# Sums of down weights moved ahead of the attention, roots and broadcasts moved forward by the scheduler, and another order in the last quarter

## The chip, the core and the metric

The kernel runs as one program on one core of a Trainium2 chip. The core has a matrix engine (TensorE, in the profile PE, with its weight loads as PEld), three engines for element-wise work (VectorE = DVE, ScalarE = ACT, GpSimd = POOL) and SyncE (SP), which here issues nearly all transfers between the chip's large memory and the core's own memory (SBUF). Matmuls write into banks of a small accumulator memory (PSUM). The metric is the device time of one execution in microseconds (us), as the median of several runs.

## What is computed

One layer of a decoder trunk on 1024 tokens of width 1024, all in fp32. Cut to what matters here:

```python
def reference(x, mem, ...):
    h = rmsnorm(x, g_mix_pre)
    y_ssm, y_gmlp = s5_group(h @ w_in...), gmlp_group(h @ w_in...)
    x = x + rmsnorm(concat(y_ssm, y_gmlp) @ w_out, g_mix_post)
    h = rmsnorm(x, g_x_pre); mem_n = rmsnorm(mem, g_mem)
    # 4 heads of 256, 256 memory tokens
    x = x + rmsnorm(softmax(q k^T / 16) v @ w_o, g_x_post)
    h = rmsnorm(x, g_ffn_pre)
    val, gate = split(causal_conv3(h @ w_up))            # 2 x 2816 columns
    x = x + rmsnorm((val * gelu(gate)) @ w_down, g_ffn_post)
    return x

def rmsnorm(x, g):
    return x * rsqrt(mean(x * x, axis=-1) + 1e-6) * g
```

## The kernel before

**Layout.** All activations lie transposed: 128 features on the partitions, tokens along the free axis. The 1024 tokens are two halves of 512 (h = 0 and 1); a tile is 128x512 fp32, 256 KB. Every fp32 product is made of three matmuls: each operand is split into a rounded high part (a cast on ACT, L131 for weights, L252 for activations) and the rest (a subtraction on DVE, L134 and L253; L253 is on POOL for some), and `mm3` (L233) multiplies high by high, high by low and low by high. So each weight tile that SP loads (L85, `raw`) needs an ACT row and a DVE row before PE can use it.

**Stages.** In order of time: the two mixers (to about 330 us of the span), the out-projection `o1` of half 0 and of half 1 (to about 428), attention of half 0 and its projection `o2`, attention of half 1 and its `o2` (to about 660), up-projection with convolution (to about 1125), down-projection by a scheme of seven products in place of eight, which needs sums of weight blocks (to about 1310), and the tail, in which the last of these products is finished in two column quarters of 256 tokens.

**Norms.** `rms` sums squares over the features by eight or four narrow matmuls against a column of ones (L278, each 128x1), DVE turns the sum into a mean (L281), and `rsqrt` makes the inverse root by an integer guess and three Newton steps (DVE L261, L263, L269, L270: ten rows in all). `bcast` spreads the root over the partitions by matmuls against the identity (L305) into the PSUM bank `st`, and ACT copies it to SBUF (L308). `post` is the step behind a projection: times gain and broadcast (DVE L723), plus the residual (POOL L724), squares (ACT L709) and their sum (POOL or DVE L710).

**Sums of weights.** `s_sums` loads four tiles of w_down for each k of 0..10 into the pool `m` (L1350), makes four sums from them on POOL (L1354) and stores these to `sd` (L1355). It is a generator. The attention takes 14 of its steps in half 0 and the last 8 in half 1, so 28 and 16 of the 44 sums.

**Attention.** For a head: `q_block` (projection by w_q), `scores` (DVE takes the maximum, L1123, scales it by the root, L1124; ACT takes the exponential, L1128; DVE divides, L1132), `turn` (PE transposes the probabilities, L1142) and `weigh` (times v). The root for half 1 is scaled at L739.

**Tail.** `one` is one product of a quarter. While the first quarter of columns (11 k x 4 b) runs, the generator `job` squares the results of half 0 and calls `finish`: norm, broadcast, eight multiplications (DVE L766), eight residual adds (POOL L767) and the stores to the output (L769). In the second quarter (4 b x 11 k) `rms` of the first quarter's columns is called at TAIL_R and its broadcast at TAIL_B; `finish_pair` (L774, L776) multiplies and adds two row blocks at a time; L1515, L1516 are the quarter's squares and their sum.

**What sets the order.** The program is written in one order, and a scheduler then sorts each engine's instructions by an estimate of when they can run, weighing in a priority, which follows the place in the program. `tc.high_priority(n)` gives what is written under it the priority of n places earlier. `self.pin(...)` keeps rows in the order of the program while `self.pinned` is set. Tiles come from pools with a fixed number of slots (here `m` 16, `t` 11, `b` 32), and an instruction that writes a slot waits until its last reader is done.

Of the kernel before, what the change touches and what calls it, by code (L numbers as in the profile page):

```python
# [19 lines left out]
ALU = mybir.AluOpType  # L20
AX = mybir.AxisListType

P = 128
D = 1024
KT = 8
HALF = 512
NG = 32
EPS = 1e-6
# [9 lines left out]
POST_A = 0.8  # L38
POST_2B = 1
S5_RATE = 1.5  # L40
WARM = 10
EARLY = 1
MIX_AT = 2
Q_STATS = 3
TAIL_R = (1, 1)
TAIL_B = (1, 9)
T_FROM = 11
T_RATE = 1
FETCH = 2
# [102 lines left out]
class Builder:  # L152
# [102 lines left out]

    def rsqrt(self, x, shape, e=None):

        v = e or self.nc.vector
        y = self.tiny(shape, f"rs_y{shape[1]}", 1 if shape[1] == 64 else 4)
        t = self.tiny(shape, f"rs_t{shape[1]}", 1)  # L260
        self.pin(v.tensor_scalar(y.bitcast(I32), x.bitcast(I32), -0.5, 1597463007.0, ALU.mult, ALU.add))  # L261
        for _ in range(3):
            self.pin(v.tensor_tensor(t, y, y, ALU.mult))  # L263
            if e:
                e.tensor_tensor(t, t, x, ALU.mult)
                e.tensor_scalar(t, t, -0.5, 1.5, ALU.mult, ALU.add)
                e.tensor_tensor(y, y, t, ALU.mult)
                continue
            self.pin(v.scalar_tensor_tensor(t, t, -0.5, x, ALU.mult, ALU.mult))  # L269
            self.pin(v.scalar_tensor_tensor(y, t, 1.5, y, ALU.add, ALU.mult))  # L270
        return y

    def rms(self, acc, nt):

        nc = self.nc
        ps = self.bank("st")
        for i in range(nt):
            self.pin(nc.tensor.matmul(ps[:, i:i + 1], lhsT=acc[:, i * P:(i + 1) * P], rhs=self.ones[:, 0:1],  # L278
                                      start=True, stop=True))
        x = self.tiny([P, nt], "st_x", 2)  # L280
        self.pin(nc.vector.tensor_scalar(x, ps[:, :nt], 1.0 / D, EPS, ALU.mult, ALU.add))  # L281
        return self.rsqrt(x, [P, nt])

    def token_rms(self, name, nt, tag):

        nc = self.nc
        ss = self.tiny([P, 2, nt], f"ss_{name}", 1)
        for i in range(nt):
            for j in range(2):
                t = self.slot(tag)  # L290
                nc.sync.dma_start(t, self.a[name][i][:, j])
                nc.scalar.activation(t, t, AF.Square, accum_out=ss[:, j, i:i + 1])
            yield
        x = self.tiny([P, nt], f"sx_{name}", 1)
        g = nc.gpsimd
        g.tensor_tensor(x, ss[:, 0], ss[:, 1], ALU.add)
        g.tensor_scalar(x, x, 1.0 / D, EPS, ALU.mult, ALU.add)
        return self.rsqrt(x, [P, nt], g)

    def bcast(self, r, nt, tag="st"):  # L300

        nc = self.nc
        ps = self.bank("st")
        for i in range(nt):
            self.pin(nc.tensor.matmul(ps[:, i * P:(i + 1) * P], lhsT=r[:, i:i + 1].to_broadcast([P, P]),  # L305
                                      rhs=self.ident, start=True, stop=True))
        bc = self.slot(tag)
        nc.scalar.copy(bc[:, :nt * P], ps[:, :nt * P])  # L308
        return ps, bc

    def stats(self, acc, nt):
# [443 lines left out]
    def finish(self, m, acc, h, x2d):  # L755

        nc, v, g = self.nc, self.nc.vector, self.nc.gpsimd
        res = []
        for i in range(KT):
            t = self.slot("rs")  # L760
            nc.sync.dma_start(t, x2d[i][h])
            res.append(t)
        r, bc = yield from self.stats(acc, 4)
        for i in range(KT):
            x = m[i]
            v.scalar_tensor_tensor(x, x, self.gain["g_ffn_post"][:, i:i + 1], bc, ALU.mult, ALU.mult)  # L766
            g.tensor_tensor(x, x, res[i], ALU.add)  # L767
            yield
            nc.sync.dma_start(self.out[P * i:P * i + P, HALF * h:HALF * h + HALF], x)  # L769

    def finish_pair(self, x, res, bc, i, h, c0, e):

# [275 lines left out]
    def attention(self):  # L1048
        nc, a, w, ids = self.nc, self.a, self.w, self.ids
        v, g = nc.vector, nc.gpsimd  # L1050
# [37 lines left out]
        sq1 = [None, None]  # L1088
        xres = lambda i, hh: a["xT"][P * i:P * i + P, HALF * hh:HALF * hh + HALF]
        post = [None, None]  # L1090
        kv = self.side(kv_parts(), 1)
        for h in range(2):
            for b in range(8):
                proj(lambda k, hh: self.mix[k, hh], "o1", m1, sq1, b, h, (4, 5, 6, 7, 0, 1, 2, 3))
            for k in range(8):
                del self.mix[k, h]
            post[h] = self.post(m1[h], sq1[h], "g_mix_post", xres, h, "q", lambda i, hh: self.x1d[i][hh])
            if h == 0:
                self.drain(kv)
                self.side(post[0])  # L1100
# [56 lines left out]
        m2 = self.m2 = [[None] * 8, [None] * 8]  # L1157
        sq2 = [None, None]
        self.post2 = [None, None]
        s_job = self.s_sums()  # L1160
        for h in range(2):
            heads = lambda k, hh: oT[hh][k]
            for i in range(6):
                if i > 1:
                    next(s_job, None)
                if i == 5:
                    for b in range(EARLY):
                        begin(heads, "o2", b, h, range(6))
                if i == 1:
                    self.drain(post[h])  # L1170
                if 1 <= i <= 4:
                    scores(h, i - 1)
                for j in range(2):
                    if i:
                        next(s_job, None)
                    if i < 4:
                        q_block(h, i, j)
                    if i >= 2:
                        turn(i - 2) if j == 0 else weigh(h, i - 2)
            self.xg[h] = []  # L1180
            if h == 0:
                self.side(post[1])
            for b in range(8):
                proj(heads, "o2", m2, sq2, b, h)
            oT[h] = None
            self.post2[h] = self.post(m2[h], sq2[h], "g_x_post", lambda i, hh: self.x1d[i][hh], h, "f",
                                      lambda i, hh: self.x2d[i][hh])
            if h == 0:
                while not self.ready[1]:
                    next(post[1])  # L1190
                self.side(self.post2[0], POST_A)
            else:
                self.drain(self.post2[0])
# [148 lines left out]
    def s_sums(self):  # L1342

        nc, g = self.nc, self.nc.gpsimd
        for k in range(11):
            t = {}
            for o in range(2):
                for j in range(2):
                    t[o, j] = self.slot("m")
                    nc.sync.dma_start(t[o, j], self.a["w_dk"][k + 11 * j][:, HALF * o:HALF * o + HALF])  # L1350
            yield

            def put(n, to, x, y, op=ALU.subtract):
                g.tensor_tensor(t[to], t[x], t[y], op)  # L1354
                nc.sync.dma_start(self.sd[n][k], t[to])  # L1355

            put(1, (1, 1), (1, 0), (1, 1), ALU.add)
            put(3, (1, 0), (0, 0), (1, 0))
            put(2, (0, 0), (1, 1), (0, 0))
            put(4, (0, 1), (0, 1), (0, 0))  # L1360
            yield
# [80 lines left out]
    def down(self):  # L1442
# [69 lines left out]
        def squares(b, q):  # L1512
# [2 lines left out]
            self.pin(nc.scalar.activation(s, A[b][:, c], AF.Square))  # L1515
            self.pin(v.tensor_tensor(sq[1][:, c], sq[1][:, c], s, ALU.add))  # L1516

        for k in range(11):
            self.d_prep(44 if k > 5 else 39 + k)
            parts.append((self.dp.pop((33 + k, 0)), self.dp.pop((33 + k, 1))))  # L1520
            for b in range(4):
                one(k, b, quarters[0])
                if k == 10:
                    squares(b, 0)
                    out_part(4 + b, 0, A[b][:, quarters[0]])
            next(job, None)
        self.drain(job)
        st = {}
        for b in range(4):
            self.pinned = b > 0  # L1530
            for k in range(11):
                one(k, b, quarters[1])
                if (b, k) == TAIL_R:
                    st["r"] = self.rms(sq[1][:, quarters[0]], 2)
                if (b, k) == TAIL_B:
                    bc = self.bcast(st["r"], 2)[1]
                    for i in (3, 2):
                        self.drain(self.finish_pair(mg[0][i], res[0][i], wide(bc), i, 1, 0, g))
                    st["out"] = self.chain(*(self.finish_pair(mg[0][i], res[0][i], wide(bc), i, 1, 0, v)
                                             for i in (0, 1)))  # L1540
                if (b, k) > TAIL_B and k % 3 == 0:
                    next(st["out"], None)
            if b == 3:
                self.drain(st["out"])
            squares(b, 1)
            out_part(4 + b, 1, A[b][:, quarters[1]])
# [77 lines left out]
```

## Time and profile before

| | us |
|---|---|
| three runs | 1373.46, 1376.73, 1373.87 |
| median | 1373.87 |
| the profiled execution | 1375.64 |
| its span | 1373.8 |
| mean granted clock of PE in it | 0.967 of full |
| PE / DVE / POOL / ACT busy | 1275.9 / 1066.1 / 694.6 / 628.0 |

The span runs from the first to the last instruction of the profiled execution; the execution's own time is 1.8 us longer. All rows of a timeline are in us from the span's start: start, duration of the group, engine, line of the kernel, operation, tile written <- tiles read, shape, and in brackets the idle time of the engine ahead of the group with the instruction that ended it. A row of the waits is: waiting engine, tile and line, the releaser, then the total, the count, and the longest. A row of the windows is: the stretch and its length, busy time of PE, PEld, DVE, ACT and POOL (with counts), the granted clock of PE, the share in which the DMA engines were busy, and GB/s.

### The profile page before, as it was taken

To read this page: it belongs to the slowest core of one execution; us is meant where nothing else is said; L and a number is where in the kernel's file an instruction comes from. 1 tells how busy PE (TensorE), PEld (TensorE's weight loads), DVE (VectorE), ACT (ScalarE), POOL (GpSimd) and SP (SyncE) were. 2 spreads that over 40 slices of the span, in tenths; PEclk is the share of its full clock that TensorE was granted. 3 is DMA by queue.
4 is the path that set the end of the run, shared out by engine and by line. 5 is a ranking of instruction groups with operands and counts; after the bars stand their busy time and mean duration, and the time that the engine had idled before them with its cause. 6 is when DMAs were issued, how large, how long until landed. Compare 5 with 4: busy or idle time off the path is not lost. (4 is left out here: it accounts for less than half of the span.)

```text
span 1373.8 us, 19246 instructions
## 1 busy us (share of the span) xinstructions
PE 1275.9 (93%) x6352; PEld 1080.4 (79%) x6352; DVE 1066.1 (78%) x1619; ACT 628.0 (46%) x1172; POOL 694.6 (51%) x532
## 2 busy tenths in 40 slices
PE   9799898779998999769999999999999999999993
PEld 7689897678886888558887878888888888788883
DVE  7968799876377757796657978888899879966576
ACT  7223331246444445345544654555555554446340
POOL 1586355834258524860343838656565227822144
PEclk9899999899998999979999999999999999999996
DMA  9654326256348844772358566545454359755123
GB/s 319 185 143 134 93 73 182 85 148 192 93 125 263 299 134 125 266 245 85 83 163 282 161 209 229 180 149 161 146 182 140 107 198 383 233 159 175 56 79 136
DMA packets 150662, 233.58 MB, mean 170 GB/s; under 512 B 33697, under 2 KB 43041, under 8 KB 150561
## 3 DMA queue, kind: packets, MB, share of 16 engines
q1 hardware_dynamic: 150560, 232.34, 53.3%
q8 instruction: 50, 0.82, 0.3%
q14 instruction: 52, 0.42, 0.1%
HBM read 174.23 MB, written 53.85 MB: 166 GB/s over the span
## 5 line engine op out<-in xcount | busy, mean ns | idle before, releaser
L233 PE MATMUL acc<-b,w 128*128 128x512 f32 x2412 | 587.9, 397 | 11.4 <-DVE b L730 4.4
L233 PEld LDWEIGHTS acc<-b,w 128*128 128x128 f32 x2412 | 457.6, 191 | 110.2 <-DVE b L730 6.5
L134 DVE TENSOR_TENSOR w<-raw,w 128x512 fp32r<-128x512 f32 x206 | 203.1, 994 | 94.2 <-PE acc L233 64.6
L233 PE MATMUL sx<-b,w 128*128 128x512 f32 x921 | 222.6, 391 | 1.7 <-ACT T L1277 1.7
L233 PEld LDWEIGHTS sx<-b,w 128*128 128x128 f32 x921 | 174.0, 189 | 38.5 <-ACT T L1277 2.1
L131 ACT CAST w<-raw 128x512 fp32r<-128x512 f32 x228 | 141.4, 622 | 125.3 <-PE acc L233 72.1
L710 POOL TENSOR_TENSOR ac<-ac,sq 128x512 f32<-128x512 f32 x52 | 78.3, 1513 | 153.2 <-ACT sq L709 152.6
L233 PE MATMUL acc<-T,w 128*128 128x512 f32 x528 | 127.0, 389 | 0.0
L233 PEld LDWEIGHTS acc<-T,w 128*128 128x128 f32 x528 | 99.1, 188 | 20.5
L253 DVE TENSOR_TENSOR w<-b,w 128x512 fp32r<-128x512 f32 x64 | 67.4, 1065 | 23.7 <-PE st L233 8.6
L1400 POOL TENSOR_TENSOR f<-f,f 128x512 f32<-128x512 f32 x33 | 55.0, 1678 | 48.1 <-DMA f<-fd 35.5
L1354 POOL TENSOR_TENSOR m<-m,m 128x512 f32<-128x512 f32 x44 | 62.8, 1432 | 31.3 <-DMA m<-in_w_dk 22.3
L724 POOL TENSOR_TENSOR m<-m,rs 128x512 f32<-128x512 f32 x32 | 49.3, 1545 | 48.6 <-DMA rs<-x1d 18.9
L233 PE MATMUL sx<-T,w 128*128 128x512 f32 x264 | 66.5, 389 | 0.0
L253 DVE TENSOR_TENSOR b<-f,b 128x512 fp32r<-128x512 f32 x53 | 54.4, 1041 | 4.3 <-ACT b L252 4.0
L233 PEld LDWEIGHTS sx<-T,w 128*128 128x128 f32 x264 | 49.6, 188 | 10.3
L709 ACT ACTIVATE sq<-m 128x512 f32<-128x512 f32 x66 | 41.3, 630 | 30.6 <-POOL m L724 13.5
L1216 POOL TENSOR_TENSOR b<-b,m 128x512 f32<-128x512 f32 x22 | 32.5, 1478 | 44.7 <-ACT m L1215 44.2
L115 POOL TENSOR_TENSOR st<-st,b 128x512 f32<-128x512 f32 x20 | 26.6, 1328 | 52.5 <-DMA st<-in_w_up 29.4
L252 ACT CAST w<-b 128x512 fp32r<-128x512 f32 x64 | 39.5, 619 | 27.3 <-PE acc L233 16.9
L233 PE MATMUL acc<-w,b 128*128 128x256 f32 x384 | 50.9, 290 | 0.0
L252 ACT CAST b<-f 128x512 fp32r<-128x512 f32 x53 | 32.7, 619 | 38.4 <-DVE w L253 34.3
(345 smaller groups left out, 2278.9 us busy)
## 6 DMA issues: line engine op xcount, KB each, us to landing
raw<-in_w_up SPq DMA_DIRECT2D x68, 256.0 KB, 3.0
f<-fd SPq DMA_DIRECT2D x55, 256.0 KB, 4.6
m<-in_w_dk SPq DMA_DIRECT2D x44, 256.0 KB, 4.7
sd<-m SPq DMA_DIRECT2D x44, 256.0 KB, 3.8
b<-sd SPq DMA_DIRECT2D x44, 256.0 KB, 4.0
b<-in_w_up SPq DMA_DIRECT2D x40, 256.0 KB, 2.8
raw<-in_w_out SPq DMA_DIRECT2D x32, 256.0 KB, 2.7
raw<-in_w_q SPq DMA_DIRECT2D x32, 256.0 KB, 3.4
```

What stands on the lines that cost most here:

```text
L115: g.tensor_tensor(p["S4"], p["12"], p["S2"], ALU.subtract)
L131: nc.scalar.copy(hi[:, :w], t[:, :w])
L134: e.tensor_tensor(lo[:, :w], t[:, :w], hi[:, :w], ALU.subtract)
L233: self.pin(nc.tensor.matmul(ps, lhsT=x, rhs=y, start=first and i + j == 0, stop=last and i == n - 1 and j == 2, skip_group_check=go_on))
L252: self.nc.scalar.copy(hi, src)
L253: (e or self.nc.vector).tensor_tensor(lo, src, hi, ALU.subtract)
L709: nc.scalar.activation(sq, src, AF.Square)
L710: (e or nc.gpsimd).tensor_tensor(acc, acc, sq, ALU.add)
L724: g.tensor_tensor(x, x, rs, ALU.add)
L1216: nc.gpsimd.tensor_tensor(val, val, gate, ALU.mult)
L1354: g.tensor_tensor(t[to], t[x], t[y], op)
L1400: self.nc.gpsimd.tensor_tensor(s[to], s[x], s[y], ALU.subtract)
```

## The change

Three things are altered.

1. Roots and broadcasts: everything in `rsqrt`, the two rows ahead of it in `token_rms`, and the matmuls and the copy in `bcast` stand under `high_priority(400)`.
2. `s_sums` is begun earlier: each of the eight projections of `o1` in half 0 takes a step, attention of half 0 takes 14 as before and drains what is left. The first four k hold their tiles in the pool `t` and not in `m`.
3. The tail: `finish` reads the broadcast from the PSUM bank and no longer from its copy, its rows are pinned, the residual adds of i = 3 and 7 are on DVE, the store is issued ahead of the yield. The steps of `job` are taken at other places (two ahead of the first quarter, one at k = 8, the rest at every even k of the second quarter's first two blocks b). The first quarter's norm uses a bank of `sx`, TAIL_R and TAIL_B move, and the whole second quarter is pinned.

```diff
+AHEAD = 400
-TAIL_R = (1, 1)
-TAIL_B = (1, 9)
+TAIL_R = (0, 7)
+TAIL_B = (1, 3)
+JOB_AT = (8,)
...
     def rsqrt(self, x, shape, e=None):
+        with self.tc.high_priority(AHEAD):
+            return self.rsqrt_(x, shape, e)
...
-    def rms(self, acc, nt):
+    def rms(self, acc, nt, bank="st"):
-        ps = self.bank("st")
+        ps = self.bank(bank)
...
-    def bcast(self, r, nt, tag="st"):
+    def bcast(self, r, nt, tag="st", bank="st"):
-        ps = self.bank("st")
-        for i in range(nt):
-            self.pin(nc.tensor.matmul(...))
+        ps = self.bank(bank)
         bc = self.slot(tag)
-        nc.scalar.copy(bc[:, :nt * P], ps[:, :nt * P])
+        with self.tc.high_priority(AHEAD):
+            for i in range(nt):
+                self.pin(nc.tensor.matmul(...))
+            nc.scalar.copy(bc[:, :nt * P], ps[:, :nt * P])
...
     # finish
-        r, bc = yield from self.stats(acc, 4)
+        r = self.rms(acc, 4)
+        yield
+        bc = self.bcast(r, 4)[0]
+        yield
         for i in range(KT):
             x = m[i]
-            v.scalar_tensor_tensor(x, x, self.gain["g_ffn_post"][:, i:i + 1], bc, ALU.mult, ALU.mult)
-            g.tensor_tensor(x, x, res[i], ALU.add)
+            self.pin(v.scalar_tensor_tensor(x, x, self.gain["g_ffn_post"][:, i:i + 1], bc, ALU.mult, ALU.mult))
+            e = v if i % 4 == 3 else g
+            self.pin(e.tensor_tensor(x, x, res[i], ALU.add))
+            nc.sync.dma_start(self.out[P * i:P * i + P, HALF * h:HALF * h + HALF], x)
             yield
-            nc.sync.dma_start(self.out[P * i:P * i + P, HALF * h:HALF * h + HALF], x)
...
     # out-projection o1 and attention
+        s_job = self.s_sums()
         for h in range(2):
             for b in range(8):
                 proj(lambda k, hh: self.mix[k, hh], "o1", m1, sq1, b, h, (4, 5, 6, 7, 0, 1, 2, 3))
+                if h == 0:
+                    next(s_job)
...
-        s_job = self.s_sums()
...
             if h == 0:
+                self.drain(s_job)
                 self.side(post[1])
...
     # s_sums
-                    t[o, j] = self.slot("m")
+                    t[o, j] = self.slot("t" if k < 4 else "m")
...
     # tail
+        next(job)
+        next(job)
         for k in range(11):
...
-            next(job, None)
-        self.drain(job)
+            if k in JOB_AT:
+                next(job)
         st = {}
+        self.pinned = True
         for b in range(4):
-            self.pinned = b > 0
             for k in range(11):
                 one(k, b, quarters[1])
+                if k % 2 == 0 and b < 2:
+                    next(job, None)
                 if (b, k) == TAIL_R:
-                    st["r"] = self.rms(sq[1][:, quarters[0]], 2)
+                    st["r"] = self.rms(sq[1][:, quarters[0]], 2, "sx")
                 if (b, k) == TAIL_B:
-                    bc = self.bcast(st["r"], 2)[1]
+                    bc = self.bcast(st["r"], 2, "st", "sx")[1]
```

Lines of the changed kernel stand some places lower: L710 becomes L718, L724 L732, L766 L777, L767 L779, L1350 L1365, L1354 L1369, L1355 L1370, L281 L287, L261 to L270 L267 to L276, L85 L87.

POOL, in the attention of half 1. Of the rows, L710 (L718) is the sum of squares for the norms (`ac`), L1354 a sum of weights. Before:

```order
L710 TENSOR_TENSOR ac_5333<-ac_5333,sq_5590 128x512
L1354 TENSOR_TENSOR m_5911<-m_5909,m_5911 128x512
L710 TENSOR_TENSOR ac_5379<-ac_5379,sq_5621 128x512
L710 TENSOR_TENSOR ac_5333<-ac_5333,sq_5644 128x512
L1354 TENSOR_TENSOR m_5909<-m_5905,m_5909 128x512
L710 TENSOR_TENSOR ac_5333<-ac_5333,sq_5686 128x512
L1354 TENSOR_TENSOR m_5905<-m_5911,m_5905 128x512
L1354 TENSOR_TENSOR m_6032<-m_6030,m_6032 128x512
L710 TENSOR_TENSOR ac_5333<-ac_5333,sq_5748 128x512
L1354 TENSOR_TENSOR m_5907<-m_5907,m_5905 128x512
```

The same stretch of POOL's rows after the change, where L732 is the residual add of `post` for half 0:

```order
L718 TENSOR_TENSOR ac_5443<-ac_5443,sq_5649 128x512
L718 TENSOR_TENSOR ac_5397<-ac_5397,sq_5654 128x512
L718 TENSOR_TENSOR ac_5443<-ac_5443,sq_5685 128x512
L718 TENSOR_TENSOR ac_5397<-ac_5397,sq_5708 128x512
L718 TENSOR_TENSOR ac_5397<-ac_5397,sq_5750 128x512
L718 TENSOR_TENSOR ac_5397<-ac_5397,sq_5812 128x512
L732 TENSOR_TENSOR m_5395<-m_5395,rs_5989 128x512
L732 TENSOR_TENSOR m_5454<-m_5454,rs_6036 128x512
```

The sums of weights between the sums of squares are gone; the residual adds follow the squares directly.

SP, in the out-projection of half 0, whose weights are `in_w_out`. Before, only weight loads stand there:

```order
L85 DMA raw_3629<-in_w_out 128x512
L85 DMA raw_3653<-in_w_out 128x512
L85 DMA raw_3675<-in_w_out 128x512
L85 DMA raw_3702<-in_w_out 128x512
L85 DMA raw_3724<-in_w_out 128x512
```

After, with loads of w_down (`t<-in_w_dk`) and stores of its sums (`sd<-t`):

```order
L87 DMA raw_3629<-in_w_out 128x512
L1370 DMA sd_1_252<-t_3805 128x512
L87 DMA raw_3653<-in_w_out 128x512
L1370 DMA sd_0_262<-t_3687 128x512
L1365 DMA t_3915<-in_w_dk 128x512
L87 DMA raw_3675<-in_w_out 128x512
L1370 DMA sd_1_241<-t_3801 128x512
L1365 DMA t_4009<-in_w_dk 128x512
L1365 DMA t_4011<-in_w_dk 128x512
L87 DMA raw_3710<-in_w_out 128x512
```

Sixteen loads and sixteen stores now share SP's queue with the weights of `o1`; each store waits for its sum on POOL.

DVE, in the tail. The rows from L281 on are the first quarter's root; `st_12982` is the copy of half 0's broadcast in SBUF. Before, the root stands behind all eight multiplications of `finish`, of which the last three are shown:

```order
L766 SCALAR_TENSOR_TENSOR m_12226<-m_12226,gains,st_12982 128x512
L766 SCALAR_TENSOR_TENSOR m_12231<-m_12231,gains,st_12982 128x512
L766 SCALAR_TENSOR_TENSOR m_12236<-m_12236,gains,st_12982 128x512
L281 TENSOR_SCALAR st_x<-st 128x2
L261 TENSOR_SCALAR rs_y_13163<-st_x 128x2
```

After, all rows of the start of `finish`:

```order
L777 SCALAR_TENSOR_TENSOR m_12201<-m_12201,gains,st 128x512
L777 SCALAR_TENSOR_TENSOR m_12206<-m_12206,gains,st 128x512
L777 SCALAR_TENSOR_TENSOR m_12211<-m_12211,gains,st 128x512
L287 TENSOR_SCALAR st_x<-sx 128x2
L267 TENSOR_SCALAR rs_y_13126<-st_x 128x2
```

and where the root ends, with a residual add (L779) now on DVE:

```order
L276 SCALAR_TENSOR_TENSOR rs_y_13126<-rs_t_13127,rs_y_13126 128x2
L777 SCALAR_TENSOR_TENSOR m_12216<-m_12216,gains,st 128x512
L779 TENSOR_TENSOR m_12216<-m_12216,rs_13004 128x512
L777 SCALAR_TENSOR_TENSOR m_12221<-m_12221,gains,st 128x512
L1531 TENSOR_TENSOR ac_11081<-ac_11081,sq_13153 128x256
```

The root has moved ahead of five of the eight multiplications, which read the PSUM bank (`st` without a number), and the root's own sum comes from a bank of `sx`.

More of the change, by code (lines that the diff above doesn't have):

```diff
@@ L256, in rsqrt, with rsqrt_ @@
     def rsqrt(self, x, shape, e=None):
+        with self.tc.high_priority(AHEAD):
+            return self.rsqrt_(x, shape, e)
+    def rsqrt_(self, x, shape, e):
         v = e or self.nc.vector
@@ L295, in token_rms @@
         g = nc.gpsimd
-        g.tensor_tensor(x, ss[:, 0], ss[:, 1], ALU.add)
-        g.tensor_scalar(x, x, 1.0 / D, EPS, ALU.mult, ALU.add)
+        with self.tc.high_priority(AHEAD):
+            g.tensor_tensor(x, ss[:, 0], ss[:, 1], ALU.add)
+            g.tensor_scalar(x, x, 1.0 / D, EPS, ALU.mult, ALU.add)
         return self.rsqrt(x, [P, nt], g)
-    def bcast(self, r, nt, tag="st"):
+    def bcast(self, r, nt, tag="st", bank="st"):
         nc = self.nc
-        ps = self.bank("st")
-        for i in range(nt):
-            self.pin(nc.tensor.matmul(ps[:, i * P:(i + 1) * P], lhsT=r[:, i:i + 1].to_broadcast([P, P]),
-                                      rhs=self.ident, start=True, stop=True))
+        ps = self.bank(bank)
         bc = self.slot(tag)
-        nc.scalar.copy(bc[:, :nt * P], ps[:, :nt * P])
+        with self.tc.high_priority(AHEAD):
+            for i in range(nt):
+                self.pin(nc.tensor.matmul(ps[:, i * P:(i + 1) * P], lhsT=r[:, i:i + 1].to_broadcast([P, P]),
+                                          rhs=self.ident, start=True, stop=True))
+            nc.scalar.copy(bc[:, :nt * P], ps[:, :nt * P])
         return ps, bc
```

## The prediction

> **What bounds the kernel now.** I read the engines' busy times first, then the waits of TensorE (PE), then PE's timeline wherever one of those waits falls, and last the windows for the granted clock.
>
> ```profile
> PE 1275.9 (93%) x6352; PEld 1080.4 (79%) x6352; DVE 1066.1 (78%) x1619; ACT 628.0 (46%) x1172; POOL 694.6 (51%) x532
> ...
> PE st L305 <- DVE rs_y L270: 14.4, 3, 11.9
> PE st L305 <- POOL rs_y L267: 8.0, 1, 8.0
> PE st L278 <- POOL ac L710: 7.4, 2, 6.5
> PE sx L1142 <- ACT t L1128: 7.1, 1, 7.1
> PE sx L233 <- ACT t L252: 4.4, 3, 3.5
> ```
>
> PE is the bound: 1275.9 of the span's 1373.8 us. The change removes no matmul, so all it can win is PE's idle 98 us and what a lowered clock costs behind an idle stretch; it can lose by new idle time. In the order of the built program PE's rows change in two places only, the second half's attention and the tail. So the 8.0 us wait for the root of x and the 6.5 us one on the first half's squares stay, and "400 places forward" acts less widely than the words say. POOL and SP change in a third place, the first half's out-projection.
>
> **Second half's attention.** Order of time, one engine after the other:
>
> ```profile
> 568.14 1.05 PE L278 MATMUL st<-ones,ac 128*128 128x1 f32 x8 [0.94 <-POOL ac L710]
> 585.97 1.11 PE L233 MATMUL sx<-kv,t 128*128 128x256 f32 x4 [3.47 <-ACT t L252]
> 591.22 1.13 PE L305 MATMUL st<-ident,rs_y 128*128 128x128 f32 x8 [0.18 <-DVE rs_y L270]
> 598.52 5.74 PE L233 MATMUL acc<-b,w 128*128 128x512 f32 x24
> 611.40 1.12 PE L1142 MATMUL sx<-ident,t 128*128 128x128 f32 x4 [7.15 <-ACT t L1128]
> ...
> 574.13 1.07 DVE L261 TENSOR_SCALAR rs_y<-st_x 128x4 int32<-128x4 int32 x1
> 582.09 0.17 DVE L739 TENSOR_SCALAR rs_y<-rs_y 128x4 f32<-128x4 f32 x1
> 594.35 9.54 DVE L723 SCALAR_TENSOR_TENSOR m<-m,gains,st 128x512 f32<-128x512 f32 x8
> ...
> 583.14 0.56 ACT L1128 ACTIVATE t<-sx,mx,rs_y 128x256 f32<-128x256 f32 x1 [10.65 <-DVE mx L1124]
> 609.63 0.56 ACT L1128 ACTIVATE t<-sx,mx,rs_y 128x256 f32<-128x256 f32 x1 [6.82 <-DVE mx L1124]
> ...
> 576.39 5.26 POOL L1354 TENSOR_TENSOR m<-m,m 128x512 f32<-128x512 f32 x4
> ```
>
> The root of the scores' scale (L261 to L739) takes 574.13 to 582.26, 8.1 us, beside POOL's weight sums (L1354). A root with POOL idle:
>
> ```profile
> 1361.92 0.17 DVE L261 TENSOR_SCALAR rs_y<-st_x 128x2 int32<-128x2 int32 x1
> 1363.69 0.16 DVE L270 SCALAR_TENSOR_TENSOR rs_y<-rs_t,rs_y 128x2 f32<-128x2 f32 x1
> ```
>
> Those ten rows take 1.93 us, with L739's 0.17 2.1. After the change the sixteen L1354 are gone from this stretch, so mx and the exponentials come about 6.0 us sooner. Terms:
> - The 0.94 us wait: POOL adds the last square without a sum ahead of it. Gone, -0.9.
> - The 3.47 us wait: the cast of t (L252) stands behind the exponentials on ACT; 6.0 is more than 3.47. Gone, -3.5.
> - The 7.15 us wait. From the broadcast (591.22) to the exponentials (609.63) are 18.4 us: 3.1 to the first L723, 9.5 for eight of them, 5.7 for the DVE rows to mx. L723 alone is 0.66 us (two in the tail start 0.66 apart), so eight take 5.3 to 9.5; POOL now has only the residual adds (L724) beside them, every third waiting for its load: 7.5. The other two become 2.6 and 4.4 with fewer POOL rows. Sum 14.5, plus 1.8 from the first exponential to the transposes (611.40 - 609.63). PE in that time did 13.0 us of work (591.22 to 604.26); the broadcast stands 13 matmuls earlier in the new order, which with full clock makes 14.0. Left: 16.3 - 14.0 = 2.3. So -4.8.
> - The clock.
>
> ```profile
> 586.00:596.00 10.00, 9.23 (x47) 7.91 (x48) 9.76 (x20) 2.92 (x6) 5.46 (x4) 0.83 0.94 325
> ...
> 611.40:618.00 6.60, 5.26 (x14) 3.91 (x15) 6.56 (x14) 4.53 (x11) 2.64 (x2) 0.50 0.90 278
> 618.00:628.00 10.00, 10.00 (x51) 8.58 (x50) 7.00 (x10) 4.22 (x9) 2.63 (x3) 0.89 0.37 131
> ...
> 1349.00:1352.00 3.00, 3.00 (x15) 3.00 (x16) 0.86 (x1) 1.12 (x3) 1.38 (x2) 0.50 0.00 0
> 1352.00:1356.00 4.00, 4.00 (x27) 4.00 (x27) 3.97 (x4) 0.00 (x0) 3.92 (x3) 0.74 0.00 0
> ```
>
> The clock column (after POOL's, 1.00 is full) falls behind each long wait: 10 x 0.17 = 1.7 us are lost behind the first, 6.6 x 0.50 + 10 x 0.11 = 4.4 behind the second. The first goes (-1.7); of the second I take half (-2.2), since 2.3 us of idle may still drop a window. The Trainium skill ("TensorE: Matmul & The Clock Gate", Why this matters for your kernels) advises against idle gaps over about 3 us, a window of which brings the clock down; by that 2.3 us would cost nothing, and the whole would be 2.2 us faster.
>
> With 0.6 for new small waits: -0.9 - 3.5 - 4.8 - 1.7 - 2.2 + 0.6 = **-12.5**. Ends: -5 if the long wait and its clock stay (first, second and fourth term, one of them halved); -20 if both are gone entirely.
>
> **The tail.** PE's last quarter, then DVE, POOL:
>
> ```profile
> 1331.78 0.91 PE st L305 x8
> ...
> 1348.86 1.19 PE L305 MATMUL st<-ident,rs_y 128*128 128x128 f32 x4 [11.94 <-DVE rs_y L270]
> 1361.09 0.61 PE L278 MATMUL st<-ones,ac 128*128 128x1 f32 x4 [0.94 <-DVE ac L1516]
> ...
> 1328.91 0.16 DVE L270 SCALAR_TENSOR_TENSOR rs_y<-rs_t,rs_y 128x4 f32<-128x4 f32 x1
> 1333.33 11.47 DVE L766 SCALAR_TENSOR_TENSOR m<-m,gains,st 128x512 f32<-128x512 f32 x8 [1.38 <-ACT st L308]
> 1344.90 1.04 DVE L261 TENSOR_SCALAR rs_y<-st_x 128x2 int32<-128x2 int32 x1
> 1365.31 1.29 DVE L774 TENSOR_TENSOR m<-m,st 128x512 f32<-128x512 f32 x2 [1.45 <-ACT st L308]
> ...
> 1334.15 12.98 POOL L767 TENSOR_TENSOR m<-m,rs 128x512 f32<-128x512 f32 x8 [9.62 <-DVE m L766]
> 1365.35 1.27 POOL L774 TENSOR_TENSOR m<-m,st 128x512 f32<-128x512 f32 x1 [8.72 <-ACT st L308]
> ...
> 1310.38 14.87 PE acc L233 x124
> ```
>
> Before, PE stands 11.94 us at the second broadcast, since its root is queued behind eight L766. A 256-wide matmul takes 14.87/124 = 0.12 us. After, step by step:
> - The first broadcast now stands 11 matmuls behind the column sums of the first half (36 earlier). PE gets there at 1327.4, the root ends at 1329.1 as before: a new wait of 1.7. Broadcast to 1330.0, copy, first multiplication at 1330.7 (1333.33 - 1332.69 = 0.64 later).
> - Three multiplications to 1332.7; the quarter's column sums on PE, 21 matmuls on, end at 1333.1. The root: 4.0 as before (two of its rows stood behind POOL then too, 1.04 each), done 1337.1. PE, 21 matmuls further, waits from 1335.6: 1.6 us in place of 11.94.
> - PE has then 0.5 + 87 x 0.12 and is done at 1348.1; its last squares allow the final column sums at 1349.0.
> - DVE from 1337.1: five multiplications at 0.66, two residual adds (i of 3 and 7, moved from POOL), four pair rows at 0.6, four square sums at 0.42: 8.6 alone. POOL has seven rows in that time; each holds up one DVE row by 1.7 - 0.65 = 1.05 at most: 16.0. Done between 1345.7 and 1353.1; with PE's floor 1349.0 to 1353.1. I take 1351.6, since the pair rows and adds read two SBUF tiles like the blocked L766, the multiplications don't: the new finish reads the broadcast from PSUM, and two L774 of that kind ran in 1.29 us inside a POOL row (1365.31 beside 1365.35).
>
> Before, 1361.09; so 9.5 sooner, less 0.5 for a low clock after PE's 3.5 us of idle: **-9.0**, ends -12 and -7. From there to the end nothing changes. The Trainium skill ("SBUF — State Buffer", Who interferes with whom) has the same rule: VectorE contends with GpSimd when it reads two SBUF inputs, not with one. If the multiplications were blocked as the eight L766 were, the term would be -7.
>
> **First half's out-projection.** Sixteen sums, loads and stores (8.4 MB) come here.
>
> ```profile
> 325.37 4.45 PE L233 MATMUL acc<-w,m 128*128 128x256 f32 x35 [0.71 <-DVE w L134]
> 315.41 9.35 POOL L253 TENSOR_TENSOR kv<-m,kv 128x512 fp32r<-128x512 f32 x6 [3.40 <-ACT kv L252]
> L1354 POOL TENSOR_TENSOR m<-m,m x44: 1264/1297/1812, 434.5 to 606.2; 128x512 f32<-128x512 f32 x44
> ```
>
> POOL then works 16 x 1.3 + 8 x 1.4 = 32 us on end from 315, and DVE's weight splits (L134) meet it. PE lost 0.71 there beside 9.35 us of POOL. Scaled to 32 us that is 2.4; but from 329.65 each split has 2.7 us of matmuls to hide behind, so **+1.5**, ends 0 and +4. On SP the stores stand ahead of weight loads, and each waits for its sum. PE's cover is the splits made ahead, three at the thinnest in the new order of ACT, 8 us; I cost it at nothing beyond that. In the first half's attention the count of sums stays 28.
>
> **Sum.** -12.5 - 9.0 + 1.5 = -20.0 on the profiled execution: 1375.64 (span 1373.8 and 1.8 around it) to 1355.6. That run stands 1.8 over the median of 1373.87, so the time is 1353.9: **1354**.
>
> **Rivals.** (1) The long wait in the second half stays, because eight L723 still go first on DVE and POOL's L724 replace the sums beside them: -20.0 + 4.8 + 2.2, 1361. For it: the order keeps the eight in one block. Against it: 9.54 us for them needed POOL busy throughout. 0.22. (2) The tail wins only what POOL's lock leaves, and the new waits add a half-clock window each: -20.0 + 6, 1360; 0.06. (3) Slower: on SP a store waits for its sum, the next weight load stands behind the store, and PE behind that load.
>
> ```profile
> m<-in_w_dk SPq DMA_DIRECT2D x44, 256.0 KB, 4.7
> ...
> 761.62 5.44 PE acc L233 x24
> ```
>
> A weight tile feeds 12 matmuls of 512 columns, 5.44/2 = 2.7 us of PE; a store holds SP for up to a landing and a sum, 4.7 + 1.3 = 6.0 us, when the load was issued just ahead. At 6.0 sixteen stores lose 16 x 3.3 = 53 us, less the 8 of cover and the 21.5 won elsewhere: 1397. It decides from 4.5 us a store on. Against it: in the new order about four weight loads, 10.8 us of PE's work, stand between a load and its own store, so the landing is over by then, and in the first half's attention the same chain runs between loads of w_q. 0.05. (4) No difference: the waits removed come back as waits for weights, 1372; 0.05.
>
> **Numbers.** The forecast holds 0.62. Below 1345 needs nearly every term at its far end; above 1366 lie (3), (4) and part of (1). A measurement of this kernel tells about 0.3% (4 us) from nothing: faster 0.90, within 0.3% 0.05, slower 0.05.
>
> **What would show it.** Right: no L1354 behind the first half's attention; the scores' root in about 2 us; PE's wait at L1142 under 4; no PE wait over 3 us before the tail's second broadcast, final column sums some 21 us sooner in the span with 9 from the tail; multiplications of 0.7 us beside POOL's adds. Wrong: PE waits on w L134 between 320 and 380 of more than 4 us, SP rows of sd stores with long gaps there, or a wait of 7 us that only moves to another row of the second half.

## The result, and the profile after

The changed kernel takes 1355.12 us (median; 1353.4 to 1358.03) beside 1375.23 us of the kernel before in the same comparison: a ratio of 0.9856, with a 95% interval of 0.9833 to 0.9879. A second comparison (e11 below) gave 1353.8 us beside 1373.04 and 0.9861 (0.9839 to 0.9882). The forecast was 1354.

The engines' busy times and some of PE's waits in the changed kernel:

```profile
PE 1274.1 (94%) x6352; PEld 1080.1 (80%) x6352; DVE 1061.4 (79%) x1621; ACT 628.1 (46%) x1172; POOL 695.2 (51%) x530
...
PE acc L235 <- DVE w L136: 8.4, 8, 2.1
PE st L314 <- POOL rs_y L273: 7.9, 2, 7.6
PE st L284 <- POOL ac L718: 5.5, 1, 5.5
...
PE sx L1157 <- ACT t L1143: 1.7, 1, 1.7
```

PE does the same work and stands idle for 77 us where it stood for 98. The single waits of 11.9 and 7.1 us are gone; the two that the prediction said would stay (7.6 for the root of x, 5.5 for the first half's squares) have stayed.

Second half's attention, changed kernel, PE, DVE, ACT and POOL apart:

```profile
567.50 0.94 PE L284 MATMUL st<-ones,ac 128*128 128x1 f32 x8
582.35 1.05 PE L314 MATMUL st<-ident,rs_y 128*128 128x128 f32 x8
598.54 0.66 PE L1157 MATMUL sx<-ident,t 128*128 128x128 f32 x4 [1.74 <-ACT t L1143]
600.11 0.50 PE L235 MATMUL sx<-kv,t 128*128 128x256 f32 x2 [0.91 <-ACT t L254]
602.03 0.58 PE L235 MATMUL sx<-kv,t 128*128 128x256 f32 x1 [1.43 <-DVE t L255]
...
572.21 0.17 DVE L267 TENSOR_SCALAR rs_y<-st_x 128x4 int32<-128x4 int32 x1
574.69 0.17 DVE L747 TENSOR_SCALAR rs_y<-rs_y 128x4 f32<-128x4 f32 x1
584.06 9.60 DVE L731 SCALAR_TENSOR_TENSOR m<-m,gains,st 128x512 f32<-128x512 f32 x8 [1.10 <-ACT st L316]
...
597.28 0.56 ACT L1143 ACTIVATE t<-sx,mx,rs_y 128x256 f32<-128x256 f32 x1
...
584.89 3.43 POOL L732 TENSOR_TENSOR m<-m,rs 128x512 f32<-128x512 f32 x2 [13.93 <-DVE m L731]
```

The waits of 0.94 and 3.47 us are gone, the scores' root takes 2.65 us (572.21 to 574.86) where it took 8.1, and the wait at the transposes is 1.74 us where it was 7.15. The eight multiplications (L731) still take 9.6 us. The granted clock, in the windows' column behind POOL's:

```profile
586.00:596.00 10.00, 10.00 (x54) 8.50 (x54) 10.00 (x10) 2.92 (x5) 6.30 (x5) 1.00 0.56 169
596.00:605.00 9.00, 4.92 (x18) 3.43 (x17) 8.93 (x20) 6.92 (x17) 2.79 (x3) 0.79 0.85 275
605.00:615.00 10.00, 10.00 (x47) 8.45 (x46) 5.39 (x8) 2.86 (x5) 1.76 (x2) 0.85 0.35 110
```

The tail of the changed kernel, PE first, then DVE and POOL:

```profile
1315.26 2.04 PE L314 MATMUL st<-ident,rs_y 128*128 128x128 f32 x8 [1.76 <-DVE rs_y L276]
1324.48 0.62 PE L314 MATMUL sx<-ident,rs_y 128*128 128x128 f32 x4
1338.88 0.99 PE L284 MATMUL st<-ones,ac 128*128 128x1 f32 x4 [3.35 <-DVE ac L1531]
...
1317.96 2.06 DVE L777 SCALAR_TENSOR_TENSOR m<-m,gains,st 128x512 f32<-128x512 f32 x3 [2.85 <-ACT st L316]
1322.05 0.16 DVE L287 TENSOR_SCALAR st_x<-sx 128x2 f32<-128x2 f32 x1 [2.02 <-PE sx L284]
1336.24 1.63 DVE L788 TENSOR_TENSOR m<-m,b 128x512 f32<-128x512 f32 x1
...
1318.79 3.75 POOL L779 TENSOR_TENSOR m<-m,rs 128x512 f32<-128x512 f32 x3 [8.24 <-DVE m L777]
```

PE comes to the second broadcast (1324.48) without a wait here; in the second profile of the same kernel (e11) it waits 1.44 us, and the part on the prediction says why. A multiplication takes 0.7 us beside POOL's adds. What PE waits for now, 3.35 us ahead of the final column sums, is VectorE with its pair rows (L786, L788) of 1.6 to 1.8 us each.

**Two stretches.** Single executions of one kernel differ by several us (17 of the kernel before, in one comparison: 1369.61 to 1379.7), so the kernels below are compared by stretches between two rows that every profile has: the attention from the last wait for b ahead of it to the weighing of the last head, the tail from the wait for m in the down-projection to the span's end. The rows of before, then of after:

```profile
556.72 10.48 PE L233 MATMUL acc<-b,w 128*128 128x512 f32 x44 [1.71 <-DVE b L730]
646.31 1.66 PE L233 MATMUL acc<-t,kv 128*128 128x512 f32 x6 [0.27 <-DVE t L253]
1188.80 5.07 PE L233 MATMUL acc<-b,w 128*128 128x512 f32 x14 [3.04 <-ACT m L1467]
```

```profile
557.43 10.22 PE L235 MATMUL acc<-b,w 128*128 128x512 f32 x38 [0.45 <-DVE b L738]
634.28 1.65 PE L235 MATMUL acc<-t,kv 128*128 128x512 f32 x6 [0.25 <-DVE t L255]
1175.05 4.86 PE L235 MATMUL acc<-b,w 128*128 128x512 f32 x14 [4.08 <-ACT m L1482]
```

That is 646.31 - 556.72 = 89.6 and 1373.8 - 1188.80 = 185.0 before, 634.28 - 557.43 = 76.9 and 1351.5 - 1175.05 = 176.4 after. All kernels by the same rows of their profiles, with the medians of their comparisons:

| kernel | median, us | before beside it | ratio (95%) | attention | tail |
|---|---|---|---|---|---|
| before | | | | 89.6 | 185.0 |
| after | 1355.12 | 1375.23 | 0.9856 (0.9833 to 0.9879) | 76.9 | 176.4 |
| after, second time (e11) | 1353.8 | 1373.04 | 0.9861 (0.9839 to 0.9882) | 76.1 | 176.9 |
| e1, sums moved only | 1359.94 | 1374.1 | 0.9897 (0.9882 to 0.9911) | 76.5 | 182.6 |
| e2, tail only | 1365.34 | 1374.1 | 0.9940 (0.9924 to 0.9956) | 89.3 | 176.8 |
| e3, priority only | 1375.0 | 1374.1 | 1.0009 (0.9995 to 1.0022) | 88.5 | 184.3 |
| e4, before without the adds | 1358.01 | 1374.1 | 0.9883 (0.9867 to 0.9899) | 75.4 | 186.3 |
| e5, after with the sums again | 1370.1 | 1373.59 | 0.9969 (0.9953 to 0.9985) | 89.7 | 175.5 |
| e6, finish from the copy | 1358.2 | 1373.59 | 0.9881 (0.9858 to 0.9903) | 77.4 | 179.1 |
| e7, late pair | 1352.48 | 1373.59 | 0.9839 (0.9815 to 0.9864) | 77.3 | 174.6 |
| e8, post from PSUM | 1339.05 | 1373.59 | 0.9745 (0.9721 to 0.9770) | 72.5 | 176.4 |
| e9, all of them | 1337.98 | 1373.04 | 0.9743 (0.9721 to 0.9765) | 71.0 | 172.9 |
| e10, before, post from PSUM | 1361.22 | 1373.04 | 0.9913 (0.9894 to 0.9933) | 85.6 | 184.4 |

Each stretch is from one profile. Where the order of the tail is the same, its stretch differs from profile to profile by up to 3.7 us in the old order (182.6 to 186.3) and 1.4 us in the new one (175.5 to 176.9, without e6, e7 and e9, which alter the tail).

### The profile page after: what moved, and what is told of

It reads as the page before. It is cut to its first block, busy times and chain, and to the rows that moved or that the text cites. A ratio compares the mean times of both kernels' runs of the same rounds, so it can differ in the third digit from the quotient of the medians.

```text
span 1351.5 us, 19229 instructions
## 1 busy us (share of the span) xinstructions
PE 1274.1 (94%) x6352; PEld 1080.1 (80%) x6352; DVE 1061.4 (79%) x1621; ACT 628.1 (46%) x1172; POOL 695.2 (51%) x530
## 4 chain that ended last, share of the span: by engine, by line
PE 53%; DVE 8%; issue 2%; DMA 1%; ACT 1%; POOL 1%; SPq 0%; DVEq 0%; ACTq 0%; POOLq 0%
PE acc L235 32%; PE sx L235 17%; PE st L235 2%; DVE w L136 1%; DVE m L731 1%; DVE w L255 1%; DVE b L255 1%; DMA rs<-x1d 1%; PE st L314 1%; POOL ac L718 0%; PE st L284 0%; DVE m L786 0%; POOL m L732 0%; DVE m L788 0%; DVE b L738 0%
## 5 line engine op out<-in xcount | busy, mean ns | idle before, releaser
L136 DVE TENSOR_TENSOR w<-raw,w 128x512 fp32r<-128x512 f32 x206 | 211.1, 1033 | 86.0 <-PE acc L235 47.1
L718 POOL TENSOR_TENSOR ac<-ac,sq 128x512 f32<-128x512 f32 x52 | 80.4, 1554 | 141.3 <-ACT sq L717 97.3
L732 POOL TENSOR_TENSOR m<-m,rs 128x512 f32<-128x512 f32 x32 | 50.0, 1570 | 62.3 <-DVE m L731 30.8
L254 ACT CAST w<-b 128x512 fp32r<-128x512 f32 x64 | 39.6, 620 | 31.0 <-PE acc L235 19.2
L1369 POOL TENSOR_TENSOR m<-m,m 128x512 f32<-128x512 f32 x28 | 39.4, 1414 | 19.6 <-DMA m<-in_w_dk 8.7
```

Of the source, the lines that this page charges most:

```text
L136: e.tensor_tensor(lo[:, :w], t[:, :w], hi[:, :w], ALU.subtract)
L254: self.nc.scalar.copy(hi, src)
L718: (e or nc.gpsimd).tensor_tensor(acc, acc, sq, ALU.add)
L732: g.tensor_tensor(x, x, rs, ALU.add)
```

## The experiments

### Each part by itself (e1, e2, e3)

e1 is before with the move of the sums:

```diff
+        s_job = self.s_sums()        # ahead of o1
...
+                if h == 0:
+                    next(s_job)
...
+                self.drain(s_job)
...
-                    t[o, j] = self.slot("m")
+                    t[o, j] = self.slot("t" if k < 4 else "m")
```

> The kernel before with the move of the weight sums alone. Theory (the sixteen POOL sums and what they hold up in the second half's attention are the cost): about 14 us less than before, some 1360 where before shows 1374; PE reaches the end of the second half's attention about 12 us sooner, the first half's out-projection is 1.5 to 2 us longer, the tail is as before with its 11.9 us wait. Rival (the roots and broadcasts under high priority make the attention shorter): at most 3 us less.

e2 is before with the new `finish`, TAIL_R, TAIL_B, JOB_AT, banks and pins, and no other part:

```diff
-            v.scalar_tensor_tensor(x, x, self.gain["g_ffn_post"][:, i:i + 1], bc, ALU.mult, ALU.mult)
+            self.pin(v.scalar_tensor_tensor(x, x, self.gain["g_ffn_post"][:, i:i + 1], bc, ALU.mult, ALU.mult))
...
-TAIL_R = (1, 1)
-TAIL_B = (1, 9)
+TAIL_R = (0, 7)
+TAIL_B = (1, 3)
```

> The kernel before with the new tail alone. Theory (the two parts touch different stages and add up): 8.4 us less than before, some 1365.5; the attention as before with its waits of 3.5 and 7.1 us, PE without a wait at the tail's second broadcast. Rival (the tail gains only because its weights and sums come earlier with the other part): less than 4 us.

e3 is before with the three `high_priority(400)`:

```diff
+        with self.tc.high_priority(AHEAD):
+            return self.rsqrt_(x, shape, e)
```

> The kernel before with roots, broadcasts and copies under high priority 400 and nothing else. Theory (the priority moves no row, since every row stands where it did): no difference, within 0.2% of before, 1374, every wait of PE as before. Rival (it is what brings the roots forward in the second half's attention): 5 to 12 us less.

e1 saves 14.2 us, e2 8.8, e3 nothing (its interval holds 1); the two that act sum to 23.0 where both together save 19 to 20, with 2 to 3 us of uncertainty in each. The attention is shortened by e1 alone and the tail by e2 alone: the tail stretches of the kernels that keep the old tail (before, e1, e3, e4, e10) lie between 182.6 and 186.3 us, with the wait of 11.9 us in each, those of the kernels with the new one between 172.9 and 179.1. The deciding waits, e1 first, then e2, then e3, each with the transposes and the tail's second broadcast:

```profile
598.12 0.66 PE L1145 MATMUL sx<-ident,t 128*128 128x128 f32 x4 [1.48 <-ACT t L1131]
1333.62 1.19 PE L305 MATMUL st<-ident,rs_y 128*128 128x128 f32 x4 [11.93 <-DVE rs_y L270]
```

```profile
611.12 1.12 PE L1151 MATMUL sx<-ident,t 128*128 128x128 f32 x4 [6.92 <-ACT t L1137]
1336.53 0.71 PE L311 MATMUL sx<-ident,rs_y 128*128 128x128 f32 x4 [1.43 <-DVE rs_y L275]
```

```profile
607.87 1.11 PE L1150 MATMUL sx<-ident,t 128*128 128x128 f32 x4 [4.78 <-ACT t L1136]
1344.89 1.19 PE L314 MATMUL st<-ident,rs_y 128*128 128x128 f32 x4 [11.94 <-DVE rs_y L276]
```

In e3 every instruction of every engine stands where it stands in before; so it does in a program built with 100,000 in the place of 400, and the changed kernel built without the priority is the same program as with it. So the first item of the change, roots and broadcasts moved forward, does nothing here. e3 therefore is a second look at the kernel before, and its profile shows how far one execution strays: a span of 1369.4 against 1373.8, and 4.78 us at the transposes against 7.15, with the same program order.

### What in the sums costs (e4, e5)

e4 is before without the last sixteen adds; loads and stores of these tiles stay:

```diff
-                g.tensor_tensor(t[to], t[x], t[y], op)
+                if k < 7:
+                    g.tensor_tensor(t[to], t[x], t[y], op)
                 nc.sync.dma_start(self.sd[n][k], t[to])
```

> The kernel before, whose last sixteen sums of weights (k of 7 to 10, second half's attention) are left out while their loads and stores stay: the stores write the loaded tiles. Theory (POOL's adds are the cost: they hold up the squares and block VectorE's rows with two SBUF inputs): 10 to 13 us less in the second half's attention, about 1362, the scores' root in 2 to 3 us. Rival (SyncE's queue and the 8 MB of traffic are the cost): less than 3 us.

e5 is the changed kernel, which repeats loads and adds of k = 7 to 10 in the second half's attention:

```diff
-    def s_sums(self):
+    def s_sums(self, again=False):
-        for k in range(11):
+        for k in range(7 if again else 0, 11):
...
-                nc.sync.dma_start(self.sd[n][k], t[to])
+                if not again:
+                    nc.sync.dma_start(self.sd[n][k], t[to])
...
+                    if h:
+                        next(again, None)
```

> The changed kernel, which loads and adds the tiles of the last four k a second time in the second half's attention and stores nothing of them. Theory (it is POOL's adds there that cost): 10 to 13 us more than the changed kernel's 1355, some 1367, with the wait at the probabilities' transposes back at 5 to 7 us and the scores' root back over 6 us. Rival (the gain came from the stores and from SyncE's queue): at most 3 us more.

e4, then e5:

```profile
596.46 0.66 PE L1142 MATMUL sx<-ident,t 128*128 128x128 f32 x4 [0.72 <-ACT t L1128]
```

```profile
594.79 1.23 PE L235 MATMUL sx<-kv,t 128*128 128x256 f32 x4 [6.00 <-ACT t L254]
617.94 1.12 PE L1158 MATMUL sx<-ident,t 128*128 128x128 f32 x4 [5.96 <-DVE ac L718]
...
580.43 1.06 DVE L267 TENSOR_SCALAR rs_y<-st_x 128x4 int32<-128x4 int32 x1
589.42 1.12 DVE L747 TENSOR_SCALAR rs_y<-rs_y 128x4 f32<-128x4 f32 x1
```

Without the adds the attention stretch is 75.4 us although SP still carries all loads and stores; with the adds back and no stores it is 89.7, the 89.6 of before, and the root takes 10.1 us (580.43 to 590.54). So the adds on POOL cost the 13 us, not the traffic. e4 saves more than was expected, 16.1 us in all and 14.2 of them in the stretch. The adds on the one hand hold up the squares in POOL's queue, on the other hand DVE's rows; e4 and e5 don't part these two. Of the 15 to 16 us that e5 is longer than the changed kernel, the stretch holds 12.8. Its profile also comes 5.4 us later to the stretch (562.82 where the changed kernel shows 557.43), but that execution, 1375.74 us, is the longest of its twelve and 5.6 above their median; whether the delay is e5's doing is open.

### The tail (e6, e7)

```diff
# e6: finish reads the copy
-        bc = self.bcast(r, 4)[0]
+        bc = self.bcast(r, 4)[1]
# e7: the second pair behind the final root
+        self.drain(late)             # finish_pair of i = 1, between rms and bcast
```

> The changed kernel, whose finish reads the broadcast's copy in SBUF in place of the PSUM bank; every row keeps its place. Theory (a VectorE row with two SBUF inputs gives way to POOL's rows, one with a PSUM input doesn't): multiplications of 1.7 us beside POOL's adds in place of 0.7, the tail 2 to 6 us longer, 1357 to 1361. Rival (the rows gain by their order alone): no difference, 1355.

> The changed kernel with the last two pair rows on VectorE (of the first quarter) moved behind the final root, where VectorE waits for the broadcast anyway. Theory (VectorE is what the final column sums wait for, 3.4 us): final column sums 1.5 to 2.4 us sooner, 1353. Rival (PE or ScalarE is the next bound at once, or the two rows come back in the last rows): within 0.5 us of the changed kernel.

The group of the eight multiplications in the list of costliest groups (busy time, mean ns of one, idle before), changed kernel and then e6, and the final column sums in e6 and in e7:

```profile
L777 DVE SCALAR_TENSOR_TENSOR m<-m,gains,st 128x512 f32<-128x512 f32 x8 | 5.6, 741 | 2.8 <-ACT st L316 2.8
```

```profile
L777 DVE SCALAR_TENSOR_TENSOR m<-m,gains,st 128x512 f32<-128x512 f32 x8 | 8.8, 1134 | 2.9 <-ACT st L316 2.9
1345.31 1.01 PE L284 MATMUL st<-ones,ac 128*128 128x1 f32 x4 [5.09 <-DVE ac L1531]
```

```profile
1339.46 0.58 PE L284 MATMUL st<-ones,ac 128*128 128x1 f32 x4 [1.95 <-DVE ac L1531]
```

With all rows in place, reading SBUF in place of PSUM lengthens a multiplication from 741 to 1134 ns and the tail by 2.7 us; the final wait grows from 3.35 to 5.09. So of the tail's 8.6 us some 2.7 come from the operand and 6 from the order, give or take what profiles differ by; the intervals of e6 and of the changed kernel overlap, so the rows show this and the times do not. In e7 the wait falls to 1.95 and the tail by 1.8 us, as expected; its median is 1 to 3 us below the changed kernel's two, less than the intervals can tell.

### The operand in PSUM (e8, e10, e9)

e8 is the changed kernel, e10 the kernel before, both with this edit in `post`; no row moves on any engine:

```diff
-        r, bc = yield from self.stats(acc, 4)
+        r = self.rms(acc, 4)
+        yield
+        yield
+        bc = self.bcast(r, 4)[0]
         yield
```

> The changed kernel, whose norms behind the projections (post) also read the first broadcast from the PSUM bank and not from the copy; every row keeps its place. Theory (two SBUF inputs are what VectorE loses beside POOL): the eight multiplications in the second half's attention take 5.3 to 6 us in place of 9.6, the exponentials come some 4 us sooner, the wait of 1.7 us at the transposes is gone and the clock with it: 2 to 5 us less, 1350 to 1353. Rival (the bank st is held by the eight rows, and the next matmul into it waits): no gain, or up to 3 us more.

> The kernel before, with the sums of weights where they were and the old tail, whose norms behind the projections read the first broadcast from PSUM; every row keeps its place. Theory (of the 7.1 us wait in the second half's attention the multiplications hold 4.2, the other sums' harm is to the small rows of the roots and to the queue of squares): 8 to 12 us less than before, 1362 to 1366, eight multiplications in under 6 us beside POOL's sums. Rival (with the sums there, POOL itself is too late and PE waits as long): less than 4 us.

e9 adds to e8 the same reading in the second multiplications of `post` and in the first quarter's pair rows on DVE, and e7's late pair:

```diff
-            r, bc2 = yield from self.stats(acc2, 4)
+            r = self.rms(acc2, 4)
...
+            bc2 = self.bcast(r, 4)[0]
...
-                    bc = self.bcast(st["r"], 2, "st", "sx")[1]
+                    ps, bc = self.bcast(st["r"], 2, "st", "sx")
...
```

> The changed kernel with every broadcast that VectorE multiplies by in the norms behind projections and in the first quarter's pair rows read from PSUM, and the late pair of the run before. Theory (two SBUF inputs are what costs beside POOL, and the savings add up): 16 us for the first reading as measured, 2.6 for the late pair, 1 to 3 for the second multiplications of the norms: 1334 to 1338. Rival (what the first reading saved was the only wait that VectorE set): 1339, as with that alone.

e11 is the changed kernel again, beside e9 and e10:

> The changed kernel as it is, for its time on the same chip: 1355 as measured, whatever the theory.

All 32 multiplications of `post`, changed kernel and then e8 (costliest groups), the latter with the eight in the second half's attention; then by shortest, median and longest in ns, before and e10, the latter with the same eight and its transposes:

```profile
L731 DVE SCALAR_TENSOR_TENSOR m<-m,gains,st 128x512 f32<-128x512 f32 x32 | 38.3, 1264 | 5.6 <-ACT st L316 5.6
```

```profile
L734 DVE SCALAR_TENSOR_TENSOR m<-m,gains,st 128x512 f32<-128x512 f32 x32 | 21.5, 743 | 5.6 <-ACT st L316 5.6
...
581.04 5.36 DVE L734 SCALAR_TENSOR_TENSOR m<-m,gains,st 128x512 f32<-128x512 f32 x8 [1.10 <-ACT st L316]
```

```profile
L723 DVE SCALAR_TENSOR_TENSOR m<-m,gains,st x32: 737/1774/1832, 390.9 to 719.6; 128x512 f32<-128x512 f32 x32
```

```profile
L726 DVE SCALAR_TENSOR_TENSOR m<-m,gains,st x32: 733/741/748, 392.2 to 706.3; 128x512 f32<-128x512 f32 x32
...
588.55 5.34 DVE L726 SCALAR_TENSOR_TENSOR m<-m,gains,st 128x512 f32<-128x512 f32 x8
601.38 0.66 PE L1145 MATMUL sx<-ident,t 128*128 128x128 f32 x4 [2.71 <-ACT t L1131]
```

Not one of 32 rows is held up any more, though POOL works beside them as before. e8 is the largest gain from a single edit: 1339.05 us, some 15 below the changed kernel, far more than the 2 to 5 expected. Between the two profiles the span shrinks by 11.1 us: 2.6 ahead of the attention stretch, 4.3 in it, 4.1 between it and the tail stretch, and 0.1 in the tail. The four `post` steps lie in the first three of these. The granted clock rises from 0.971 to 0.976, by estimate worth at most 7 us (0.029 x 1351.5 - 0.024 x 1340.4), which is not apart from these parts; more was not tried. e10 saves 11.8 us of the kernel before, 4.0 of it in the attention stretch, where the wait falls from 7.15 to 2.71 us: about what eight freed multiplications make up (9.54 to 5.34).

This also tells what the 13 us of the sums are not. With the multiplications freed on both sides, e10 and e8 are still 85.6 - 72.5 = 13.1 us apart in the stretch, as before and after are (12.7); and moving the sums left the eight multiplications as they were, 9.54 us before and 9.60 after. Taken out or put back in place the sums do tell on them (7.47 us in e4, 11.53 in e5), but in the move the residual adds (L732) take the sums' place beside them. So the 4 us that freed multiplications are worth, with the sums or without, come on top of what the move gains. What the move gains lies in the rest: the roots (8.1 us for the scores' root before, 2.65 after), the squares behind the sums in POOL's queue, and the clock; these were not tried one by one. e9 has the shortest tail (172.9 us) and the shortest time, 1337.98, but its interval and e8's overlap: the times do not part the two, nor e9's theory from its rival.

## Why the prediction was right

**The sum.** Forecast -20.0 us, measured -20.1 and -19.2 by the medians. By stage:

| term | forecast | measured in the profiles |
|---|---|---|
| second half's attention | -12.5 | -12.7 (89.6 to 76.9) |
| tail | -9.0 | -8.6 (185.0 to 176.4) |
| first half's out-projection | +1.5 | +1.2 |

The third is PE's busy time from 315 to 355 us, before and after, 39.19 to 38.00 of 40:

```profile
sum 40.00, PE 39.19 PEld 34.30 DVE 20.70 ACT 22.93 POOL 15.80; mean PE 19.60 PEld 17.15 DVE 10.35 ACT 11.47 POOL 7.90
```

```profile
sum 40.00, PE 38.00 PEld 32.70 DVE 28.20 ACT 21.57 POOL 39.59; mean PE 19.00 PEld 16.35 DVE 14.10 ACT 10.78 POOL 19.80
```

The spans differ by 22.3, 2.2 more than the terms; e3 shows that one execution strays by that much.

**Attention.** The small waits of 0.9 and 3.5 went as worked out. Of the long one 2.3 us were to be left; 1.74 are, and that is in part luck. From the broadcast to the exponentials 14.5 us were forecast and 14.9 measured (582.35 to 597.28), but by two errors that cancel: the eight multiplications were to take 7.5 us and took 9.6, with the residual adds on POOL beside half of them, while the steps ahead and behind took 1.7 and 3.6 in place of 2.6 and 4.4. So rival 1 had the mechanism right (L732 takes the sums' place beside L731) and the result wrong, and what was said against it, that 9.54 us "needed POOL busy throughout", does not hold: POOL was busy for 6.30 of the 10 us from 586. The clock was to give back 3.9 us. Before, 6.1 were lost (1.7, 3.3 and 1.1 in the three windows); after, 9 x 0.21 + 10 x 0.15 = 3.4 are: 2.7 back. The Trainium skill ("TensorE: Matmul & The Clock Gate", Why this matters for your kernels) advises against idle gaps over about 3 us, and by that nothing would have been lost here; behind three waits of 1.74, 0.91 and 1.43 us within 5.2 us the clock fell all the same. How far it falls is not fixed by the waits: in the second profile (e11), with 1.80 in the place of 1.74, the same two windows read 0.83 and 0.98, a loss of 1.7 us and not 3.4.

**Tail.** The new wait ahead of the first broadcast is 1.76 us (forecast 1.7). For what follows, the second profile of the changed kernel (e11) shows what was forecast and the first does not. The clock behind the broadcast in the first and then in e11, and e11's rows of DVE and PE:

```profile
1315.00:1318.00 3.00, 2.74 (x13) 2.77 (x14) 0.15 (x2) 0.59 (x1) 0.00 (x0) 0.50 0.02 5
```

```profile
1314.00:1317.00 3.00, 2.64 (x23) 2.67 (x24) 1.03 (x4) 0.59 (x1) 0.03 (x1) 1.00 0.02 5
...
1318.57 0.97 DVE L267 TENSOR_SCALAR rs_y<-st_x 128x2 int32<-128x2 int32 x1
...
1322.39 0.71 PE L314 MATMUL sx<-ident,rs_y 128*128 128x128 f32 x4 [1.44 <-DVE rs_y L276]
```

In e11 the clock stays full, the quarter's root begins beside POOL's adds, two of its rows are held up, it takes 3.95 us (1318.38 to 1322.33; forecast 4.0), and PE waits 1.44 us at the second broadcast (forecast 1.6; 1.43 in e2). In the first profile the clock falls to half behind the same wait of 1.76 us. PE comes later to the quarter's column sums, POOL's adds end at 1322.54 and only the first of the root's rows stand beside them, so the root takes 2.3 us and PE does not wait. Both ways come to the same end, tail stretches of 176.4 and 176.9, since VectorE and not PE sets it, as worked out: final column sums at 1338.88 + 13.75 (1188.80 - 1175.05) = 1352.6 in before's time, forecast 1351.6. The Trainium skill's rule ("SBUF — State Buffer", Who interferes with whom) is that two SBUF inputs contend with GpSimd and, outside VectorE's two-port modes, one doesn't. The multiplications agree with it in e6 (741 against 1134 ns) and e8 (743 against 1264); the root's first row L267 reads one SBUF tile and is held up (0.97 us above), and no trace here shows in which mode it ran.

**Out-projection and the other rivals.** SP's queue did not become the bound (rival 3). In the changed kernel PE's waits for weights from 320 us on are 0.72, 0.60 and 0.58 us where before had one of 0.71, and 50 us of matmuls follow the last without another:

```profile
331.34 50.88 PE L235 MATMUL acc<-b,w 128*128 128x512 f32 x223 [0.58 <-DVE w L136]
```

Rival 4 did not come about. Of rival 2 the half-clock stretch behind a new wait did come in the changed kernel's first profile, but cost no time at the end of the tail.

**What was missed.** The prediction saw that the priority acts "less widely than the words say"; it acts nowhere (e3). And it expected the blocked multiplications to shorten when POOL's sums left (9.5 to 7.5 us). They did not, since the residual adds took the sums' place, and an edit that moves no work at all brings them to 5.4 (e8), with the sums beside them as well (5.3, e10).

## What to carry to other kernels

Where VectorE's rows that read SBUF stand beside GpSimd's, look at shortest, median and longest duration of one line: 0.74 beside 1.77 us was the sign here that GpSimd held rows up, and a broadcast left in PSUM took the hold away without moving anything. Move GpSimd's bulk work to a stage where VectorE has slack, as the out-projection had (20.7 of 40 us busy before). Compare the order of instructions before believing that a priority moved something, and compare stretches between two rows common to both profiles rather than spans.

## What was not expected of the hardware

- A VectorE row with a PSUM operand is not held up at all beside POOL: 32 rows between 733 and 748 ns (e10), where the same rows with two SBUF operands took 737 to 1832 with POOL's sums beside them. A blocked row lost about 1 us in both sizes seen: 737 ns became 1774 for 512 columns, 0.17 us became 1.06 for 4 (the first row of the root, changed kernel and e5).
- Rows with a single SBUF input were held up too: the root's first row (L267, `rs_y<-st_x`) and the scaling of the scores' root (L747, `rs_y<-rs_y`) took 1.06 and 1.12 us in e5 and 0.17 each in the changed kernel. So it is the operand in PSUM that is shown to help, not one SBUF operand less.
- The clock fell behind three waits, none longer than 1.74 us, and in the tail behind one of 1.76 us, in one profile of the changed kernel and not in the other.
- Reading the bank directly did not start VectorE earlier: L777 begins at 1317.96, when ScalarE's copy of the same bank ends (1317.93).
